# Paged key caches laid out with keys transposed, gathered page by page into the operand of the score matmuls

## The chip, the cores and the metric

The kernel runs on one core of a Trainium2 chip. The metric is the device time of one execution in microseconds (us). Several executions are timed, and their median is given; one more execution is recorded by the hardware profiler, and the rows below come from it. TensorE is called PE (its weight loads PEld), VectorE DVE, ScalarE ACT, GpSimd POOL, and SyncE SP; SP and POOL issue the DMAs.

## The reference, cut to what matters

One layer of a decoder handles a prompt of 512 tokens and 8 sample sequences of 4 new tokens, which share all weights. Two mixers run from one input projection: a gated short convolution, and sparse attention with three branches. What the change touches is the attention of the sample tokens over the paged past, and the state of the convolution:

```
rows   = cache_sel[page_table]            # 8 sequences x 8 pages x 128 tokens, keys and values, 4 heads of 64
s_s    = q . k_sel - slope * distance     # scores of the selected branch; one block of 64 tokens is masked out
o_s    = softmax(s_s) . v_sel
s_w    = q . k_win - slope * distance     # scores of the window branch over cache_win, 512 tokens
o_w    = softmax(s_w) . v_win
o      = gate0 * o_c + gate1 * o_s + gate2 * o_w
v      = bias + sum_k w[k] * up[t + k]    # up = state_conv (2 rows of 1024 channels) followed by cg * xin
```

All data are float32; `cache_sel` is (80 pages, 128 tokens, 2 x 4 x 64), `cache_win` (8, 512 tokens, 2 x 4 x 64), `state_conv` (8, 2, 1024).

## The kernel before, in words

The whole program is traced in order by `build`, and a scheduler orders each engine's queue; each engine then runs its queue in that order. Matmuls of the large projections take float32 operands that are split in a high and a low part (`split`: ACT makes `wh`, DVE makes `wl`), three matmuls for each block of 128 input channels (lines 181 to 183). The weights come through three buffers `raw` by DMAs on SP, and two buffers each of `wh` and `wl`.

After the projections of the queries (tiles `qh` and `ql`, stored to DRAM by SP), the stage of the sample attention begins. Its constants `tb` and the convolution state `st` are loaded by SP. Eight small PE transposes turn `st` into `stT`, channels on partitions (lines 727 to 733). Then two streams of work are woven together:

- the filler, `fill_gen`: for each of 8 channel blocks the three projections `cg`, `xin` and `bg` of the convolution (`conv_gen`), then three gate projections. It yields after every twelve matmuls (a step), four steps to a projection, 108 steps in all. Four of them run ahead of the sample attention.
- `sample_gen(bp)`, for each of 4 pairs of sequences. What it yields is the number of filler steps that are put in at that point.

For one pair, `sample_gen` first gathers the selected rows: one indirect DMA on POOL for each sequence (`gather`, line 789) fills a tile `sraw` of 128 partitions x 8 rows x 512, each partition with eight consecutive tokens (16 KB). There are two such buffers, and the window rows `wraw` use one of them later. The compressed scores (`sx`) give the importance `imp`, from which `mk` and the bias table `bs` follow; `bs` is made on POOL.

`branch` then does one branch of attention. `key_T` transposes the keys on PE (`kt`, line 850), 128 x 128 at a time with four transposes to a PSUM tile, and ACT or DVE copies the tile to SBUF. Four matmuls with the block diagonal queries `qbd` give the scores `ss`; `softmax_part` adds the table and takes the minimum; ACT does the exponential; DVE scales `S`; PE transposes the probabilities (`pt`), and matmuls with the value half of `sraw` or `wraw` add to `sacc`. The selected branch goes first, the window branch second; `wraw` is loaded between the two, by two DMAs on POOL. The yields of a pair add up to 27 steps.

PSUM tiles for projections and transposes share five buffers of tag `g`; scores have two buffers, the accumulator one. Small copies of the convolution (`up`, `ncv`) run on POOL.

Of the kernel before, what the change touches and what calls it, by code (L numbers as in the profile page):

```python
# [9 lines left out]
F32 = mybir.dt.float32  # L10
# [8 lines left out]
D = 1024  # L19
KC = 8  # L20
# [25 lines left out]
def _tables():  # L46
# [12 lines left out]
    offs = (p % 16)[:, None]  # L59
# [13 lines left out]
    pos = 8 * (n % 128) + n // 128  # L73
    tsel = -sl * (PAST + tt - pos)
    n = np.arange(512)
    pos = 512 + 4 * (n % 128) + n // 128
    wd = PAST + tt - pos
# [22 lines left out]
def build(tc, a, o):  # L100
# [52 lines left out]
    ixs = cst.tile([128, 8], I32, name="ixs")  # L153
# [203 lines left out]
    fidx = mp.tile([128, 12], F32, name="fidx")  # L357
# [15 lines left out]
    mk8 = tsm[:, 19:27].rearrange("p (x m) -> p x m", x=1).broadcast_to([128, 8, 8])  # L373
    dve.tensor_mul(pm_.rearrange("p (b x) -> p b x", b=8), ptf.rearrange("p (b x) -> p b x", b=8), mk8)
    dve.tensor_reduce(fidx[:, 4:12], pm_.rearrange("p (b x) -> p b x", b=8), axis=AX.X, op=ALU.add)
    dve.tensor_scalar(ixs, fidx[:, 4:12], 16.0, tsm[:, 2:3], ALU.mult, ALU.add)
# [399 lines left out]
    csv = a["cache_sel"].rearrange("n t w -> (n t w)").rearrange("(x y) -> x y", y=8 * 512)  # L776

# [7 lines left out]
    def gather(bp):  # L785
        res = []
        for b2 in range(2):
            t = srp.tile([128, 8, 512], F32, tag="sraw", bufs=2, name=nm("sraw"))
            pool.indirect_dma_start(out=t.rearrange("p j w -> p (j w)"), out_offset=None, in_=csv, in_offset=bass.IndirectOffsetOnAxis(ap=ixs[:, 2 * bp + b2:2 * bp + b2 + 1], axis=0))
            res.append(t)  # L790
        return res

    def sample_gen(bp):

        b0 = 2 * bp
        sraw = gather(bp)
# [23 lines left out]
        yield 3  # L820
# [17 lines left out]
        for jh in range(2):  # L838
            pool.tensor_tensor(bs[:, jh * 512:(jh + 1) * 512].rearrange("p (j s k) -> p j s k", j=4, s=16),
                               t_sel[:, jh * 512:(jh + 1) * 512].rearrange("p (j s k) -> p j s k", j=4, s=16),  # L840
                               mk.rearrange("p (x s y) -> p x s y", x=1, y=1).broadcast_to([128, 4, 16, 8]), op=ALU.add)
        dve.tensor_scalar_mul(px[:, 0:63], px[:, 0:63], G[:, 0:1])

        def key_T(raw, j0, which):

            res = []
            for b2, gp, rows in quads[2 * which:2 * which + 2]:
                tp = tp_ps(nm("kt"))
                for j in range(4):
                    pe.transpose(tp[:, j * 128:(j + 1) * 128], raw[b2][:, j0 + j, gp * 128:(gp + 1) * 128], ident)  # L850
                kt = smp.tile([128, 512], F32, tag="kt", bufs=4, name=nm("kt"))
                evac(kt, tp)
                res.append(kt)
            return res
# [3 lines left out]
        def branch(raw, nj, tables, xo, br, first):  # L858
# [3 lines left out]
            kts = key_T(raw, 0, 0)  # L862
            yield 1
            kts += key_T(raw, 0, 1)
            yield 1
            for q4 in range(k):
                p = s_ps(nm("ss"))
                for (b2, gp, rows), kt in zip(quads, kts):
                    pe.matmul(p[rows, :], lhsT=qbd[:, b0 + b2, gp, :], rhs=kt, start=True, stop=True)
                softmax_part(S[:, q4 * 512:(q4 + 1) * 512], p, tables[q4], nx[:, q4:q4 + 1])  # L870
                if q4 + 1 < k:
                    kts = key_T(raw, 4 * (q4 + 1), 0)
                    yield 1
                    kts += key_T(raw, 4 * (q4 + 1), 1)
                    yield 1
# [12 lines left out]
            yield 4  # L888
# [8 lines left out]
            yield 1  # L897
            for j in range(nj):
                for b2, gp, rows in quads:
                    pe.matmul(acc[rows, 0:128], lhsT=pts_[j // 4][:, (j % 4) * 128 + rows.start:(j % 4) * 128 + rows.stop],  # L900
                              rhs=raw[b2][:, j, 256 + gp * 128:256 + gp * 128 + 128], start=(first and j == 0), stop=False)
# [13 lines left out]
        yield 1  # L915
# [4 lines left out]
        yield 1  # L920
# [508 lines left out]
def _arrays(inputs):  # L1429
    arrs = {k: np.ascontiguousarray(np.asarray(inputs[k])).reshape(s) for k, s in _SHAPES.items()}  # L1430
    arrs["tab_s"], arrs["tab_a"], arrs["tab_b"] = _tables()
    return arrs
# [14 lines left out]
```

## Time and profile before

| | us |
|---|---|
| median of 3 runs | 1344.76 |
| lowest and highest of the runs | 1344.42, 1345.23 |
| profiled execution, its own time | 1343.75 |
| its span in the trace | 1342.0 |
| PE busy | 1310.5 |
| DVE, ACT, POOL busy | 654.3, 537.5, 70.3 |

The time of an execution holds a little more than the span of the trace: 1.75 us here. All points of time in the rows count from the start of the span. "Idle before" in a row is the time in which the engine did nothing ahead of the instruction, with what ended it.

### The profile page before, as it was taken

Reading aid. Unit: us, or ns where it says so; the run is one execution under the profiler, and the core shown is the slowest. Engines: PE = TensorE matmul, PEld = TensorE weight load, DVE = VectorE, ACT = ScalarE, POOL = GpSimd, SP = SyncE. Lnnn points to the kernel's source line nnn. Section 1 sums busy time; section 2 is a strip of 40 time slices with the busy share of each in tenths; the row PEclk is TensorE's granted clock in tenths of the full one; section 3 lists DMA queues with packets and bytes.
Section 4 is the critical chain, followed back from the end, with each engine's and each line's share of the span. In section 5 each row is a group of like instructions: output and inputs, shape, how many; then the busy total and the mean of one; then the engine's idle time right before and its main releaser. Section 6 shows DMA issues by size and latency. Waiting matters only on the chain.

```text
span 1342.0 us, 25662 instructions
## 1 busy us (share of the span) xinstructions
PE 1310.5 (98%) x10840; PEld 1210.6 (90%) x10840; DVE 654.3 (49%) x1570; ACT 537.5 (40%) x1065; POOL 70.3 (5%) x123
## 2 busy tenths in 40 slices
PE   7999999997999999999999999999999999999997
PEld 6788899996999999899777777999999999999996
DVE  5559332343454454426687676667433333333335
ACT  6335233432332334324776776435323223222223
POOL 2101030001011110001000000000000000000000
PEclk8999999998999999999999999999999999999999
DMA  9996036872535562754457336532223223133221
GB/s 330 313 331 231 33 112 188 275 218 83 215 130 196 185 213 95 195 132 131 124 152 199 101 110 176 155 126 64 64 64 95 95 65 124 56 87 87 87 64 67
DMA packets 138025, 193.56 MB, mean 144 GB/s; under 512 B 4818, under 2 KB 124762, under 8 KB 132919
## 3 DMA queue, kind: packets, MB, share of 16 engines
q1 hardware_dynamic: 133302, 149.98, 36.5%
q0 software_dynamic: 4608, 41.95, 8.3%
q8 instruction: 85, 1.39, 0.5%
q14 instruction: 30, 0.24, 0.1%
HBM read 174.47 MB, written 25.76 MB: 149 GB/s over the span
## 4 chain that ended last, share of the span: by engine, by line
PE 95%; DMA 2%; DVE 1%; ACT 1%; issue 0%; SPq 0%; ACTq 0%; DVEq 0%
PE lin L181 19%; PE lin L182 19%; PE lin L183 19%; PE dn L181 3%; PE dn L182 3%; PE dn L183 3%; PE acc L1133 3%; PE ptp L1139 3%; PE phi L462 2%; PE phi L460 2%; PE phi L461 2%; PE xt L446 2%; PE modp L229 2%; PE kt L850 2%; PE sp L1108 1%; PE sp L1109 1%
## 5 line engine op out<-in xcount | busy, mean ns | idle before, releaser
L181 PE MATMUL lin<-h_hi,wh 128*128 128x288 f32 (+1 forms) x1648 | 479.4, 291 | 0.0
L182 PE MATMUL lin<-h_lo,wh 128*128 128x288 f32 (+1 forms) x1648 | 475.2, 289 | 0.0
L183 PE MATMUL lin<-h_hi,wl 128*128 128x288 f32 (+1 forms) x1648 | 473.8, 288 | 0.0
L181 PEld LDWEIGHTS lin<-h_hi,wh 128*128 128x128 f32 x1648 | 311.1, 189 | 9.4 <-issue 8.1
L182 PEld LDWEIGHTS lin<-h_lo,wh 128*128 128x128 f32 x1648 | 310.7, 189 | 0.5
L183 PEld LDWEIGHTS lin<-h_hi,wl 128*128 128x128 f32 x1648 | 310.1, 188 | 0.3
L177 DVE TENSOR_TENSOR wl<-raw,wh 128x1024 fp32r<-128x1024 f32 x132 | 159.9, 1212 | 244.5 <-ACT wh L176 244.2
L176 ACT ACTIVATE wh<-raw 128x1024 fp32r<-128x1024 f32 x132 | 137.9, 1045 | 300.0 <-PE lin L182 211.4
L181 PE MATMUL dn<-f_hi,wh 128*128 128x256 f32 (+1 forms) x352 | 101.9, 290 | 0.0
L182 PE MATMUL dn<-f_lo,wh 128*128 128x256 f32 (+1 forms) x352 | 101.3, 288 | 0.0
L183 PE MATMUL dn<-f_hi,wl 128*128 128x256 f32 (+1 forms) x352 | 101.0, 287 | 0.0
L1115 ACT ACTIVATE P<-P,nms 128x512 f32<-128x512 f32 (+3 forms) x128 | 70.6, 555 | 18.8 <-DVE nms L1114 17.9
L1114 DVE CUSTOM_DVE_ANT_0 P<-sp,ta 128x512 f32<-128x512 f32 (+3 forms) x128 | 57.5, 482 | 31.0 <-PE sp L1102 23.5
L183 PEld LDWEIGHTS dn<-f_hi,wl 128*128 128x128 f32 x352 | 66.3, 188 | 0.0
L181 PEld LDWEIGHTS dn<-f_hi,wh 128*128 128x128 f32 x352 | 66.2, 188 | 0.0
L182 PEld LDWEIGHTS dn<-f_lo,wh 128*128 128x128 f32 x352 | 66.2, 188 | 0.0
L460 PE MATMUL phi<-xh,wph 128*128 128x512 f32 x128 | 54.0, 422 | 0.0
L461 PE MATMUL phi<-xh,wpl 128*128 128x512 f32 x128 | 52.1, 407 | 0.0
L462 PE MATMUL phi<-xl,wph 128*128 128x512 f32 x128 | 52.0, 408 | 0.0
L448 ACT ACTIVATE xh<-xt 128x512 fp32r<-128x512 f32 x64 | 34.8, 597 | 32.3 <-PE xt L446 31.4
L449 DVE TENSOR_TENSOR xl<-xt,xh 128x512 fp32r<-128x512 f32 x64 | 41.0, 684 | 13.1 <-ACT xh L448 13.1
L1139 PEld LDWEIGHTS ptp<-ident,P 128*128 128x128 f32 x320 | 35.7, 141 | 10.9 <-issue 8.9
(370 smaller groups left out, 2110.2 us busy)
## 6 DMA issues: line engine op xcount, KB each, us to landing
raw<-in_w_in SPq DMA_DIRECT2D x26, 1024.0 KB, 6.6
raw<-in_w_ada SPq DMA_DIRECT2D x24, 1024.0 KB, 9.3
raw<-in_w_gate SPq DMA_DIRECT2D x11, 1024.0 KB, 5.4
raw<-in_w_up SPq DMA_DIRECT2D x11, 1024.0 KB, 5.4
wraw<-in_cache_win POOLq DMA_DIRECT2D x8, 1024.0 KB, 7.0
raw<-in_w_down SPq DMA_DIRECT2D x8, 1024.0 KB, 5.7
out_new_win_sample<-in_cache_win SPq DMA_DIRECT2D x8, 1016.0 KB, 10.5
rq<-in_w_in SPq DMA_DIRECT2D x8, 512.0 KB, 12.0
```

What stands on the lines that cost most here:

```text
L176: act.activation(oh, view, AF.Copy)
L177: dve.tensor_sub(ol, view, oh.bitcast(F32))
L181: pe.matmul(p, lhsT=wh[:, k, :], rhs=xh, start=start, stop=False)
L182: pe.matmul(p, lhsT=wh[:, k, :], rhs=xl, start=False, stop=False)
L183: pe.matmul(p, lhsT=wl[:, k, :], rhs=xh, start=False, stop=stop)
L449: dve.tensor_sub(xlb[v][:, lp * 512:lp * 512 + 512], p, xo.bitcast(F32))
L460: pe.matmul(po, lhsT=w_h, rhs=mh, start=first, stop=False)
L461: pe.matmul(po, lhsT=w_l, rhs=mh, start=False, stop=False)
L462: pe.matmul(po, lhsT=w_h, rhs=ml, start=False, stop=last)
L1114: dve.tensor_tensor_reduce(out=t[:, 0:n], in0=sps[br], in1=t_dist[:, 512 - n:512], scale=-hs, scalar=3e38, op0=ALU.add, op1=ALU.min, accum ...
L1115: act.activation(t[:, 0:n], t[:, 0:n], AF.Exp, scale=-1.0, bias=nms[:, c:c + 1], accum_out=sums[:, c:c + 1])
L1139: pe.transpose(tp[:, r * 128:(r + 1) * 128], P[br, r][:, 128 * j:128 * j + 128], ident)
```

## The change

The host lays three inputs out in another way before the launch. In `cache_sel` a page keeps its 128 rows of 512 numbers, but row p of a page now holds, for two pairs of heads, component p of the keys of all 128 tokens (2 x 128 numbers), and then the 256 value numbers of token p. A new input `cache_winT` has the same for the window: 1024 key numbers by component, 1024 value numbers by token. `cache_win` stays for the copy to the output. `state_conv` comes as 128 x 128, channels on partitions.

In the kernel the state is loaded straight into `stT`, and the tile `st`, the eight transposes and the copy go. `gather` issues one indirect DMA for each page, eight for a sequence, 128 rows of 2 KB each. `key_T`, its transposes and the copies to `kt` go; the score matmuls read slices of `sraw` (four pages, 128 numbers each, 2 KB apart) and of the window tile as their moving operand. The position tables follow the new order of tokens. There are three buffers of tag `sraw` instead of two: the gather of a pair is issued in the middle of the pair before, after its selected branch, and that of the first pair ahead of the filler; the window tile of a pair is loaded by one DMA at the pair's start. The yields of a pair are set anew and add up to 24 steps.

```diff
-    ixs = cst.tile([128, 8], I32, name="ixs")
+    ixs = cst.tile([128, 64], I32, name="ixs")
...
-    mk8 = tsm[:, 19:27].rearrange("p (x m) -> p x m", x=1).broadcast_to([128, 8, 8])
-    dve.tensor_mul(pm_.rearrange("p (b x) -> p b x", b=8), ptf.rearrange("p (b x) -> p b x", b=8), mk8)
-    dve.tensor_reduce(fidx[:, 4:12], pm_.rearrange("p (b x) -> p b x", b=8), axis=AX.X, op=ALU.add)
-    dve.tensor_scalar(ixs, fidx[:, 4:12], 16.0, tsm[:, 2:3], ALU.mult, ALU.add)
+    dve.tensor_scalar(ixs, ptf, 128.0, tsm[:, 2:3], ALU.mult, ALU.add)
...
-    st = cv.tile([16, D], F32, name="st")
-    sync.dma_start(st, a["state_conv"])
     stT = cv.tile([128, 8, 16], F32, name="stT")
-    p = tp_ps("stp")
-    for k in range(KC):
-        pe.transpose(p[:, k * 16:(k + 1) * 16], st[:, k * 128:(k + 1) * 128], ident[0:16, 0:16])
-    dve.tensor_copy(stT, p[:, 0:128].rearrange("p (k n) -> p k n", k=8))
+    sync.dma_start(stT.rearrange("p k n -> p (k n)"), a["state_conv"])
...
     def gather(bp):
         res = []
         for b2 in range(2):
-            t = srp.tile([128, 8, 512], F32, tag="sraw", bufs=2, name=nm("sraw"))
-            pool.indirect_dma_start(out=t.rearrange("p j w -> p (j w)"), out_offset=None, in_=csv, in_offset=bass.IndirectOffsetOnAxis(ap=ixs[:, 2 * bp + b2:2 * bp + b2 + 1], axis=0))
+            t = srp.tile([128, 8, 512], F32, tag="sraw", bufs=3, name=nm("sraw"))
+            for pg in range(8):
+                col = (2 * bp + b2) * 8 + pg
+                pool.indirect_dma_start(out=t[:, pg, :], out_offset=None, in_=a["cache_sel"], in_offset=bass.IndirectOffsetOnAxis(ap=ixs[:, col:col + 1], axis=0))
             res.append(t)
         return res
+    rows_of = {0: gather(0)}
...
-        sraw = gather(bp)
+        sraw = rows_of.pop(bp)
+        wt = srp.tile([128, 2, 2048], F32, tag="sraw", bufs=3, name=nm("wraw"))
+        pool.dma_start(wt, a["cache_winT"][b0:b0 + 2].rearrange("b p w -> p b w"))
...
-        yield 3
+        yield 4
...
-        def key_T(raw, j0, which):
-            res = []
-            for b2, gp, rows in quads[2 * which:2 * which + 2]:
-                tp = tp_ps(nm("kt"))
-                for j in range(4):
-                    pe.transpose(tp[:, j * 128:(j + 1) * 128], raw[b2][:, j0 + j, gp * 128:(gp + 1) * 128], ident)
-                kt = smp.tile([128, 512], F32, tag="kt", bufs=4, name=nm("kt"))
-                evac(kt, tp)
-                res.append(kt)
-            return res
...
-        def branch(raw, nj, tables, xo, br, first):
+        def branch(keys, vals, nj, tables, xo, br, first, wait):
...
-            kts = key_T(raw, 0, 0)
-            yield 1
-            kts += key_T(raw, 0, 1)
-            yield 1
             for q4 in range(k):
                 p = s_ps(nm("ss"))
-                for (b2, gp, rows), kt in zip(quads, kts):
-                    pe.matmul(p[rows, :], lhsT=qbd[:, b0 + b2, gp, :], rhs=kt, start=True, stop=True)
+                for b2, gp, rows in quads:
+                    pe.matmul(p[rows, :], lhsT=qbd[:, b0 + b2, gp, :], rhs=keys(b2, gp, q4), start=True, stop=True)
                 softmax_part(S[:, q4 * 512:(q4 + 1) * 512], p, tables[q4], nx[:, q4:q4 + 1])
-                if q4 + 1 < k:
-                    kts = key_T(raw, 4 * (q4 + 1), 0)
-                    yield 1
-                    kts += key_T(raw, 4 * (q4 + 1), 1)
-                    yield 1
...
-            yield 4
+            yield wait
...
-            yield 1
+            yield 2
...
-        yield from branch(sraw, 8, [bs[:, 0:512], bs[:, 512:1024]], 64, 1, True)
-        wt = srp.tile([128, 2, 4, 512], F32, tag="sraw", bufs=2, name=nm("wraw"))
-        wr = []
-        for b2 in range(2):
-            pool.dma_start(wt[:, b2], a["cache_win"][b0 + b2].rearrange("(p j) w -> p j w", j=4))
-            wr.append(wt[:, b2])
-        yield 6
-        yield from branch(wr, 4, [t_win], 96, 2, False)
+        yield from branch(lambda b2, gp, q4: sraw[b2][:, 4 * q4:4 * q4 + 4, gp * 128:(gp + 1) * 128],
+                          lambda b2, gp, j: sraw[b2][:, j, 256 + gp * 128:384 + gp * 128],
+                          8, [bs[:, 0:512], bs[:, 512:1024]], 64, 1, True, 6)
+        if bp < 3:
+            rows_of[bp + 1] = gather(bp + 1)
+        yield from branch(lambda b2, gp, q4: wt[:, b2, gp * 512:(gp + 1) * 512],
+                          lambda b2, gp, j: wt[:, b2, 1024 + j * 256 + gp * 128:1152 + j * 256 + gp * 128],
+                          4, [t_win], 96, 2, False, 6)
...
-        yield 1
+        yield 2
...
-        yield 1
+        yield 2
```

## Rows read from the trace of the kernel before

**Rows 1.** The page: busy time and share of PE; chain that ended last, by engine.
```profile
PE 1310.5 (98%) x10840; PEld 1210.6 (90%) x10840; DVE 654.3 (49%) x1570; ACT 537.5 (40%) x1065; POOL 70.3 (5%) x123
...
PE 95%; DMA 2%; DVE 1%; ACT 1%; issue 0%; SPq 0%; ACTq 0%; DVEq 0%
```

**Rows 2.** Windows: length, busy us by engine (instructions), clock, DMA share, GB/s.
```profile
305.00:316.00 11.00, 2.30 (x25) 2.13 (x14) 3.05 (x13) 2.84 (x5) 0.20 (x1) 0.64 0.45 153
...
440.00:497.00 57.00, 56.54 (x542) 51.96 (x541) 27.99 (x74) 18.70 (x34) 6.62 (x15) 1.00 0.53 186
497.00:545.00 48.00, 45.70 (x439) 40.91 (x438) 24.23 (x55) 23.18 (x38) 3.63 (x6) 1.00 0.32 112
```

**Rows 3.** Timeline of PE at the stage's start: start, duration, instruction, idle before.
```profile
304.84 0.29 PE L807 MATMUL sx<-kn,qbd 128*32 128x64 f32 x8
313.83 1.03 PE L732 MATMUL stp<-ident,st 16*128 16x16 f32 x8 [8.70 <-DMA st<-in_state_conv]
314.80 0.61 PE L181 MATMUL lin<-h_hi,wh 128*128 128x288 f32 x1
...
318.30 0.29 PE L183 MATMUL lin<-h_hi,wl 128*128 128x288 f32 x1
318.43 0.29 PE L181 MATMUL lin<-h_hi,wh 128*128 128x288 f32 x1
```

**Rows 4.** Timelines of ACT, DVE and SP's queue over the same stretch.
```profile
298.72 1.06 ACT L176 ACTIVATE wh<-raw 128x1024 fp32r<-128x1024 f32 x1 [2.21 <-PE lin L182]
304.70 1.06 ACT L176 ACTIVATE wh<-raw 128x1024 fp32r<-128x1024 f32 x1 [2.21 <-PE lin L182]
...
313.90 0.35 ACT L816 ACTIVATE px<-sxs,n 128x63 f32<-128x63 f32 x1 [6.48 <-DVE n L779]
...
313.44 0.28 DVE L801 TENSOR_TENSOR gm<-tb,gT 48x128 f32<-48x128 f32 x1 [5.91 <-DMA tb<-in_tab_b]
...
308.44 0.39 SPq L728 DMA_DIRECT2D st<-in_state_conv  x1
```

**Rows 5.** Chain of 316 to 545 us: shares by line, and one link.
```profile
by line: PE lin L181 23.8%; PE lin L182 22.7%; PE lin L183 22.3%; PE kt L850 9.3%; PE ss L869 5.4%; DMA sraw<-in_cache_sel,ixs 5.3%; PE sacc L900 4.6%; PE pt L893 2.3%; ACT L991 0.6%; PE imp L823 0.4%; issue 0.4%; PE ptx L912 0.4%; PE sacc 
...
327.67 1.03 PE kt L850 x8
```

**Rows 6.** PE's groups of line 850, 316 to 545 us: count, busy us, mean ns, idle.
```profile
L850 PE MATMUL kt<-ident,sraw 128*128 128x128 f32 x128 | 17.1, 276 | 0.5 <-DMA sraw<-in_cache_sel,ixs 0.5
...
L850 PE MATMUL kt<-ident,wraw 128*128 128x128 f32 x64 | 8.3, 272 | 0.0
```

**Rows 7.** POOL's groups by line over the whole span, same columns.
```profile
L428 POOL DMA_INDIRECT gt<-in_cache_cmp,ixc x16 | 16.0, 1002 | 113.4 <-DVE gt L438 111.2 <-DVE ixc L372 1.8 <-issue 0.3
...
L789 POOL DMA_INDIRECT sraw<-in_cache_sel,ixs x8 | 9.7, 1213 | 19.3 <-PE ptx L912 16.8 <-issue 1.4 <-DMA k_dr1l<-kl 0.6
L839 POOL TENSOR_TENSOR bs<-tb,mk 128x512 f32<-128x512 f32 x8 | 8.5, 1075 | 25.4 <-DVE mk L836 21.5 <-PE lin L182 3.8
```

**Rows 8.** Timelines of POOL and of DVE around two indirect DMAs.
```profile
6.93 0.96 POOL L428 DMA_INDIRECT gt<-in_cache_cmp,ixc  x1 [0.30 <-issue]
...
408.57 1.87 POOL L789 DMA_INDIRECT sraw<-in_cache_sel,ixs  x1 [0.54 <-issue]
...
408.32 1.23 DVE L177 TENSOR_TENSOR wl<-raw,wh 128x1024 fp32r<-128x1024 f32 x1 [0.53 <-ACT wh L176]
```

**Rows 9.** DMA issues: count, KB each, median us from issue to landing.
```profile
k_dr1h<-kh SPq DMA_DIRECT2D x2, 256.0 KB, 2.0
...
sraw<-in_cache_sel,ixs POOLq DMA_INDIRECT x8, 11.0
```

**Rows 10.** Timelines of DVE and PE from the mask to the scaled probabilities, pair 0.
```profile
329.63 0.24 DVE L836 TENSOR_SCALAR mk<-tb,mn 128x16 f32<-128x16 f32 x1
...
338.40 1.06 PE L869 MATMUL ss<-kt,qbd 128*32 128x512 f32 x8
...
342.79 0.75 DVE L886 TENSOR_SCALAR S<-S,f 128x1024 f32<-128x1024 f32 x1
```

More of the change, by code (lines that the diff above doesn't have):

```diff
@@ L58, in _tables @@
     offc = ((p % 8) * 4)[:, None]
-    offs = (p % 16)[:, None]
+    offs = p[:, None]
     m16 = np.arange(16)[None, :] == p[:, None] // 8
@@ L72, in _tables @@
     n = np.arange(1024)
-    pos = 8 * (n % 128) + n // 128
-    tsel = -sl * (PAST + tt - pos)
+    tsel = -sl * (PAST + tt - n)
     n = np.arange(512)
-    pos = 512 + 4 * (n % 128) + n // 128
-    wd = PAST + tt - pos
+    wd = PAST + tt - (512 + n)
     twin = np.where(wd < 512, -sl * wd, NEG)
@@ L356, in build @@
     pm_ = mp.tile([128, 64], F32, name="pm_")
-    fidx = mp.tile([128, 12], F32, name="fidx")
+    fidx = mp.tile([128, 4], F32, name="fidx")
     vrow = mp.tile([104, 128], F32, name="vrow")
@@ L774, in slab_for @@
         return conv_w[nme]
-    csv = a["cache_sel"].rearrange("n t w -> (n t w)").rearrange("(x y) -> x y", y=8 * 512)
     def softmax_part(out, pin, table, nmx):
@@ L838, in sample_gen @@
         for jh in range(2):
[L839 to L841 removed]
+            pool.tensor_tensor(bs[:, jh * 512:(jh + 1) * 512].rearrange("p (s k) -> p s k", s=8),
+                               t_sel[:, jh * 512:(jh + 1) * 512].rearrange("p (s k) -> p s k", s=8),
+                               mk[:, jh * 8:jh * 8 + 8].rearrange("p (s y) -> p s y", y=1).broadcast_to([128, 8, 64]), op=ALU.add)
         dve.tensor_scalar_mul(px[:, 0:63], px[:, 0:63], G[:, 0:1])
[L844 to L854 removed]
         acc = acc_ps(nm("sacc"))
[L858 removed]
+        def branch(keys, vals, nj, tables, xo, br, first, wait):
             S = smp.tile([128, 1024], F32, tag="S", bufs=1, name=nm("S"))
@@ L900, in branch @@
                     pe.matmul(acc[rows, 0:128], lhsT=pts_[j // 4][:, (j % 4) * 128 + rows.start:(j % 4) * 128 + rows.stop],
-                              rhs=raw[b2][:, j, 256 + gp * 128:256 + gp * 128 + 128], start=(first and j == 0), stop=False)
-        yield from branch(sraw, 8, [bs[:, 0:512], bs[:, 512:1024]], 64, 1, True)
-        wt = srp.tile([128, 2, 4, 512], F32, tag="sraw", bufs=2, name=nm("wraw"))
-        wr = []
-        for b2 in range(2):
-            pool.dma_start(wt[:, b2], a["cache_win"][b0 + b2].rearrange("(p j) w -> p j w", j=4))
-            wr.append(wt[:, b2])
-        yield 6
-        yield from branch(wr, 4, [t_win], 96, 2, False)
+                              rhs=vals(b2, gp, j), start=(first and j == 0), stop=False)
+        yield from branch(lambda b2, gp, q4: sraw[b2][:, 4 * q4:4 * q4 + 4, gp * 128:(gp + 1) * 128],
[6 more added lines that the diff above has]
+                          4, [t_win], 96, 2, False, 6)
         tp = tp_ps(nm("ptx"))
@@ L1431, in _arrays @@
     arrs["tab_s"], arrs["tab_a"], arrs["tab_b"] = _tables()
+    cs = arrs["cache_sel"].reshape(80, 128, 2, 2, 128)
+    arrs["cache_sel"] = np.concatenate([cs[:, :, 0].transpose(0, 3, 2, 1).reshape(80, 128, 256), cs[:, :, 1].reshape(80, 128, 256)], axis=2).reshape(80 * 128, 512)
+    cw = arrs["cache_win"].reshape(8, 512, 2, 2, 128)
+    cv = cw[:, :, 1].reshape(8, 4, 128, 256).transpose(0, 2, 1, 3).reshape(8, 128, 1024)
+    arrs["cache_winT"] = np.concatenate([cw[:, :, 0].transpose(0, 3, 2, 1).reshape(8, 128, 1024), cv], axis=2)
+    arrs["state_conv"] = np.ascontiguousarray(arrs["state_conv"].reshape(16, 8, 128).transpose(2, 1, 0)).reshape(128, 128)
     return arrs
```

## The prediction

> **What bounds the kernel now.** I read the page's busy shares and its chain first [rows 1]. The reader is to see one engine: TensorE (PE) is busy for 1310.5 of 1342.0 us and carries 95% of the chain that ended last. So an edit pays what it takes off PE, plus the PE idle time that it closes; work taken from VectorE, ScalarE or POOL pays only through these two. Then the windows over the stage that the diff touches, the sample attention with the convolution's matmuls as filler, 305 to 545 us [rows 2]: between 305 and 316 us PE works 2.3 of 11 us, from 440 to 497 all but 0.46 us, from 497 to 545 all but 2.3 us. Third, the timelines of that hole [rows 3, 4] and the stage's chain [rows 5]. Last, the rows of what the diff multiplies, POOL's DMAs [rows 7 to 9].
>
> The hole is a DMA's. PE finishes L807 at 305.1 us, then stands 8.7 us until state_conv has landed, because the eight transposes of `st` are next in its queue; the first projection matmul follows at 314.80 us [rows 3]. That DMA was issued at 308.44 us, behind the last q stores on SP [rows 4].
>
> **The change, part by part.**
>
> *State transposes go.* The first matmul of conv 0 can follow L807: its `wh` split had run at 298.72 us [rows 4]. That is 314.80 - 305.13 = 9.7 us. The hole also left PE at its lower level: the granted clock of 305 to 316 is 0.64 [rows 2], and the fourteen matmul intervals from 314.80 to 318.30 took 3.5 us where the pace afterwards is 0.13 us each, 1.8 us [rows 3]. Without the idle time that 1.7 us goes too: 11.4 us together. What is late next? The table `tb` lands at 313.4 us as before, and `px` on ScalarE waits for it until 313.90 [rows 4]. Behind `px` in ScalarE's queue stand the copy of `cg` and the split of the `bg` weights. PE meanwhile has `cg` and `xin` (8 steps of twelve matmuls, 1.5 us each at the 0.12 to 0.13 us pace, 12 us), whose weights were split before 306 us, so it is fed until about 317; the five PSUM tiles of tag g hold the four halves of these two. `stT` now comes by the one SP DMA and is first read for `v` of conv 0, after `xin`. Bounds of this term: 11.4 us if nothing new blocks, about 0 if `cg` is blocked just as long. I take 11.4, since the releases wanted before 317 us come at 313.4 to 313.9.
>
> *Key transposes go.* 192 transposes and 48 evacuations. In the chain of 316 to 545 us they are 9.3% of 229 us, 21.3 us, in groups of eight such as the 1.03 us at 327.67 [rows 5]; one group of about 0.9 us is hidden there behind the gather's link. PE's own busy time for them is 17.1 + 8.3 = 25.4 us [rows 6]. So between 22.2 and 25.4; I take 23. All of it counts, because the filler around them is PE work as well. The evacuations cost PE nothing before (other filler ran) and return nothing.
>
> *The score matmuls stay*: the same number, at 5.4% of 229 us [rows 5], 12 groups of 1.03 us. Their moving operand is now 128-element runs 2 KB apart instead of one run. No row shows that form; lower bound 0, upper bound a doubling, 12 us. I take 0: the value matmuls already read such slices of the same tiles, and fetch no more per column.
>
> *Steps between waits.* Per pair the generator yields 24 steps instead of 27. Of 108 filler steps 104 were left, fewer than 4 x 27, so the last pair ran out of filler; 4 x 24 = 96 leaves 8. The 2.3 us of idle time in 497 to 545 us, mostly waits for `pts` and `ob` with no filler left, and the 0.46 us before [rows 2] should close but for a few tenths: 2.3 us taken together.
>
> *The gather* is where the change can lose. One indirect DMA for each sequence becomes eight, so 16 for a pair. It is issued when the previous pair's value matmuls free the tiles, and it is needed at the next pair's first score matmul. Between lie 16 steps (24 us) and about 3.4 us of the window branch and small matmuls: 27.4 us. An indirect DMA of 128 rows holds POOL 1.00 us at 8 KB a row and 1.21 us at 16 KB [rows 7], so I bound one of 2 KB a row by 0.96 and 1.87 us, the shortest and the longest that stand in [rows 8], and add 0.30 us between two in a row [rows 8]. It is nearest to the 8 KB row, 1.0 us. Then 16 x 1.3 = 21 us, and three or so stretched by 0.86 us (below), 2.6 us. The last then lands about 2 us later, as stores of the same 256 KB do, and not after the 11 us of a 2 MB one [rows 9]: some 26 us. That fits, with 1.5 us to spare. At the upper bound, 16 x 2.17 + 2 = 37 us, each of three pairs waits 9 us. I put 0.7 us for each, 2 us. Pair 0 is fetched long before. Queued behind the 16 on POOL are the small copies of `up` and `ncv`, wanted one conv (18 us) later, then the load of `wt` and `bs`, wanted later than the gather itself; those have room if it has.
>
> Why some are stretched: the 1.87 us one at 408.57 began while VectorE's L177, started at 408.32, was running [rows 8]. [...]
>
> *Shorter room for the softmax.* Without transposes the scores follow `imp` at once, and `bs` (two POOL instructions of 1.08 us [rows 7]) comes after `mk`, which ended at 329.87, 2.2 us after `imp` gave way to the first transposes at 327.67 [rows 5, 10]. From there to the scaled `S` it is what followed the scores before, 338.40 + 1.06 to 343.54 = 4.1 us [rows 10]: 2.2 + 2.2 + 4.1 = 8.5 us against 2 + 6 x 1.5 = 11 us of cover. Two foreign instructions of 1.2 us on VectorE or ScalarE use that up; from 0 to 3 us for each of four pairs, I take 0.5: 2 us. [...] Index arithmetic at the start: three small VectorE instructions become one, under the first loads: 0.
>
> **Sum.** 11.4 + 23 + 2.3 = 36.7 us off, 2 + 2 + 1 = 5 us on: 31.7 us. The profiled execution's span of 1342.0 becomes 1310.3, its time of 1343.75 (1.75 us beside the span) becomes 1312.1. It lay 1.0 us under the median of the three runs, 1344.76; so about 1313 us.
>
> **Rivals.**
> 1. *The first hole moves instead of closing.* `cg` or the split of `bg` blocks PE for as long. For it: ScalarE stood idle 6.48 us and VectorE 5.91 us for the same `tb` [rows 4]. Against: PE has 12 us of ready matmuls. Price 9 to 11 us: 1323. Chance 0.10.
> 2. *Gather or softmax a little late*, 4 to 5 us for each pair: indirect DMAs of 1.5 to 1.9 us. For it: the stretched row. Against: 1.0 us is the common one. Price 15 us: 1328. Chance 0.13.
> 3. *Slower than before: the gather is serial.* If each DMA's landing holds up the next, one costs 1.0 us of issue and 2.0 us of landing [rows 7, 9]: 48 us, 21 us late; PE waits in order, three times, 62 us in all: 1375. It decides from the point where the waits eat 31.7 us, a gather of 38 us, 2.4 us for one DMA. Against it: two gathers stood 0.30 us apart, the first long from landed [rows 8]. Chance 0.06.
> [...]
> 4. *Strided reads cost.* The doubling above: 1325. Chance 0.02. *Nothing moves*, gains and waits cancelling: 0.03.
>
> **Chances and range.** Forecast 0.66, around 1306 to 1320: all gains with no loss give 1306, and 25.4 instead of 23 another 2 less. A measurement of this kernel can tell about 0.2%, 2.7 us. Faster than that: 0.66 + 0.10 + 0.13 + 0.02 = 0.91; same 0.03; slower 0.06. The range takes in rivals 1, 2 and 4: 1303 to 1329.
>
> **What would show it.** The projection matmuls start near 305 us with no wait for state_conv, and the clock near 1.0 from there. No `kt` rows; PE busy some 25 us less. Sixteen indirect DMAs of about 1.0 us in a row on POOL, the last landing before the next `ss`; if PE waits for `sraw`, rival 2 or 3. `ss` still 1.0 us for eight. The prediction is wrong if a gather takes over 30 us, or if PE stops behind `cg`.

## The result: slower in the first comparison, near the forecast on three chips later

The comparison that answers the prediction gave 1364.35 us (1363.85 to 1364.62) for the changed kernel against 1344.86 us for the one before: a ratio of 1.0145, with a 95% interval of 1.0127 to 1.0162. The forecast was 1313 us. So both its direction and its range were missed.

The same program, without a letter changed, was run three more times beside the kernel before, on three chips: 1316.52, 1316.95 and 1316.62 us, with ratios of 0.9797 [0.9780, 0.9813], 0.9799 [0.9783, 0.9816] and 0.9795 [0.9776, 0.9815]. The kernel before took 1344.1 to 1344.9 us everywhere. It isn't known whether the chip of the first comparison is one of them. So there are two profiles of one program to read, and the question became what lies between them: 1362.5 us of span in the first, 1315.0 us in the second.

The page of the changed kernel in the first comparison: busy time and share of PE, VectorE, ScalarE and POOL, and the chain that ended last by engine.

```profile
PE 1301.3 (96%) x10640; PEld 1200.7 (88%) x10640; DVE 636.3 (47%) x1543; ACT 521.2 (38%) x1039; POOL 121.7 (9%) x175
...
PE 94%; issue 2%; DMA 1%; DVE 1%; ACT 0%; SPq 0%; DVEq 0%; ACTq 0%
```

The same two lines where it took 1316.5 us.

```profile
PE 1285.9 (98%) x10640; PEld 1190.7 (91%) x10640; DVE 636.0 (48%) x1543; ACT 521.0 (40%) x1039; POOL 122.1 (9%) x175
...
PE 96%; DMA 1%; DVE 1%; ACT 0%; issue 0%; SPq 0%; DVEq 0%; ACTq 0%
```

Beside [rows 1] the second page is the one that was forecast: 200 matmuls fewer, PE's busy time 1310.5 - 1285.9 = 24.6 us lower. (PE's eight state transposes are among the 200.) In the first, "issue" has 2% of the chain. That word means that PE waited for nothing that the profile shows. The waits of PE say how much of it there is (line, what it waited for, us in all, times, longest).

```profile
PE lin L179 <- issue: 11.9, 13, 1.6
PE lin L180 <- issue: 10.7, 13, 1.8
PE lin L181 <- issue: 6.8, 8, 1.7
PE lin L180 <- DVE yin_lo L210: 6.1, 1, 6.1
...
PE lin L179 <- ACT yin_hi L209: 1.7, 1, 1.7
...
PE pt L867 <- issue: 1.1, 2, 0.9
```

No wait names `sraw`: the gathers were not late. 11.9 + 10.7 + 6.8 + 1.1 = 30.5 us of idle time have no cause that the profile shows. The windows say where it lies (length, PE busy, and, third from the end, the granted clock). First the run of 1364 us.

```profile
229.00:252.00 23.00, 18.02 (x131) 16.75 (x128) 4.25 (x6) 5.43 (x8) 17.28 (x17) 0.93 0.82 266
252.00:280.00 28.00, 26.98 (x193) 26.18 (x193) 8.48 (x14) 11.94 (x17) 0.10 (x1) 0.88 0.83 250
330.00:385.00 55.00, 47.34 (x433) 43.68 (x430) 21.68 (x65) 11.29 (x22) 19.98 (x27) 0.91 0.53 173
385.00:440.00 55.00, 45.81 (x426) 41.17 (x425) 21.41 (x61) 13.66 (x25) 19.44 (x27) 0.91 0.53 173
440.00:497.00 57.00, 48.97 (x447) 44.36 (x446) 22.13 (x67) 13.10 (x24) 20.02 (x28) 0.91 0.51 167
```

And the run of 1316.5 us, where all five stretches are full, at full clock; three of them:

```profile
229.00:252.00 23.00, 23.00 (x199) 22.87 (x194) 7.40 (x10) 10.62 (x16) 17.31 (x18) 1.00 0.93 294
...
330.00:385.00 55.00, 55.00 (x578) 50.60 (x577) 27.36 (x78) 16.26 (x32) 22.86 (x32) 1.00 0.65 208
...
440.00:497.00 57.00, 57.00 (x563) 53.01 (x555) 26.45 (x74) 17.66 (x31) 9.51 (x20) 1.00 0.56 177
```

The four gathers lie in just these stretches (POOL's first indirect DMAs start at 230.06, 345.99, 403.44 and 461.71 us). The span differs by 1362.5 - 1315.0 = 47.5 us. Of these 30.5 us are issue idle time, and 1301.3 - 1285.9 = 15.4 us are PE busy for longer with the same 10640 matmuls: the clock reads 0.88 to 0.93 over these stretches. In short windows around the second stall it is 1.00 up to 361 us, 0.50 from 363 to 371 us and 1.00 again from 372 us; PE's first stop of over 1 us there is that before 358.08 us. The other 1.6 us are idle time elsewhere.

One stall from close by, timelines of the run of 1364 us: POOL's row of indirect DMAs, then PE.

```profile
345.99 1.05 POOL L780 DMA_INDIRECT sraw<-in_cache_sel,ixs  x1 [10.32 <-PE sacc L874]
...
357.38 0.95 POOL L780 DMA_INDIRECT sraw<-in_cache_sel,ixs  x1 [0.30 <-issue]
...
365.66 0.95 POOL L780 DMA_INDIRECT sraw<-in_cache_sel,ixs  x1 [0.30 <-issue]
```

```profile
358.08 0.28 PE L179 MATMUL lin<-h_hi,wh 128*128 128x256 f32 x1 [1.14 <-issue]
...
360.20 0.28 PE L179 MATMUL lin<-h_hi,wh 128*128 128x256 f32 x1 [1.60 <-issue]
360.92 0.28 PE L180 MATMUL lin<-h_lo,wh 128*128 128x256 f32 x1 [0.44 <-issue]
362.32 0.37 PE L181 MATMUL lin<-h_hi,wl 128*128 128x256 f32 x1 [1.12 <-issue]
363.72 0.37 PE L179 MATMUL lin<-h_hi,wh 128*128 128x256 f32 x1 [1.03 <-issue]
...
368.65 0.37 PE L180 MATMUL lin<-h_lo,wh 128*128 128x256 f32 x1 [0.33 <-issue]
```

These are plain filler matmuls; the profile shows nothing that they wait for, and at full clock they follow each other every 0.12 us. From about the ninth DMA of the row until three us after the last has begun, PE lets through one matmul, or two or three, and mostly goes on only 0.7 us or a multiple of it later (360.20, 360.92, 362.32, 363.72). The first eight disturb nothing: PE is busy for all of 345 to 355 us.

PE isn't the only engine that is late. The copy of the tile `pt` on VectorE starts at 368.84 us, 11.9 us after the last matmul that fills it; in the run of 1316.5 us it starts 0.1 us after. PE and VectorE, the run of 1364 us, then the other:

```profile
356.66 0.27 PE L867 MATMUL pt<-ident,S 128*128 128x128 f32 x1 [0.24 <-issue]
368.84 0.69 DVE L140 COPY pts<-pt 128x512 f32<-128x512 f32 x1 [6.81 <-remote]
```

```profile
345.43 0.60 PE L867 MATMUL pt<-ident,S 128*128 128x128 f32 x4
346.14 0.68 DVE L140 COPY pts<-pt 128x512 f32<-128x512 f32 x1
```

"Remote" stands where the view can name no instruction as the releaser. In the run of 1364 us VectorE and ScalarE have nine waits of this kind, 77.8 us in all; the trace of the kernel before has none.

### The profile page after: what moved, and what is told of

The parts are those of the page before. It is cut to its first block, busy times and chain, and to the rows that moved or that the text cites. A ratio compares the mean times of both kernels' runs of the same rounds, so it can differ in the third digit from the quotient of the medians.

```text
span 1362.5 us, 25289 instructions
## 1 busy us (share of the span) xinstructions
PE 1301.3 (96%) x10640; PEld 1200.7 (88%) x10640; DVE 636.3 (47%) x1543; ACT 521.2 (38%) x1039; POOL 121.7 (9%) x175
## 3 DMA queue, kind: packets, MB, share of 16 engines
q0 software_dynamic: 8512, 41.95, 9.0%
## 4 chain that ended last, share of the span: by engine, by line
PE 94%; issue 2%; DMA 1%; DVE 1%; ACT 0%; SPq 0%; DVEq 0%; ACTq 0%
PE lin L179 19%; PE lin L181 19%; PE lin L180 19%; PE dn L180 3%; PE dn L179 3%; PE dn L181 3%; PE acc L1107 3%; PE ptp L1113 3%; PE phi L457 2%; PE phi L456 2%; PE phi L455 2%; PE xt L441 2%; PE modp L227 2%; PE sp L1082 1%; PE sp L1083 1%
## 5 line engine op out<-in xcount | busy, mean ns | idle before, releaser
L179 PE MATMUL lin<-h_hi,wh 128*128 128x288 f32 (+1 forms) x1648 | 481.1, 292 | 12.0 <-issue 11.9
L180 PE MATMUL lin<-h_lo,wh 128*128 128x288 f32 (+1 forms) x1648 | 478.8, 291 | 10.7 <-issue 10.7
L181 PE MATMUL lin<-h_hi,wl 128*128 128x288 f32 (+1 forms) x1648 | 479.6, 291 | 7.0 <-issue 6.8
L179 PEld LDWEIGHTS lin<-h_hi,wh 128*128 128x128 f32 x1648 | 314.5, 191 | 19.2 <-issue 15.4
L181 PEld LDWEIGHTS lin<-h_hi,wl 128*128 128x128 f32 x1648 | 313.6, 190 | 10.4 <-issue 10.1
L175 DVE TENSOR_TENSOR wl<-raw,wh 128x1024 fp32r<-128x1024 f32 x132 | 159.1, 1206 | 251.4 <-ACT wh L174 247.5
L780 POOL DMA_INDIRECT sraw<-in_cache_sel,ixs x64 | 64.0, 999 | 51.9 <-PE sacc L874 32.5
```

Of the source, the lines that this page charges most:

```text
L175: dve.tensor_sub(ol, view, oh.bitcast(F32))
L179: pe.matmul(p, lhsT=wh[:, k, :], rhs=xh, start=start, stop=False)
L180: pe.matmul(p, lhsT=wh[:, k, :], rhs=xl, start=False, stop=False)
L181: pe.matmul(p, lhsT=wl[:, k, :], rhs=xh, start=False, stop=stop)
L780: pool.indirect_dma_start(out=t[:, pg, :], out_offset=None, in_=a["cache_sel"], in_offset=bass.IndirectOffsetOnAxis(ap=ixs[:, col:col + 1] ...
```

## The experiments

The theories. **S**: rows of indirect DMAs hold PE's issue up, by themselves. **D**: late data or bytes do it. **C**: the chip decides whether it happens at all. **L**: a second loss, in the layout, takes 7.8 us everywhere. Kernels of one line of the table ran on that chip side by side; the first comparison's chip isn't known, and each of the five stands in one line alone.

| chip | kernels, median us |
|---|---|
| A | e1_state 1332.73, e2_once 1327.18, e3_direct 1317.36, e4_spread 1344.92 |
| B | e5_eight_wait 1316.69, e6_paced 1316.31, e7_half_row 1339.68, e8_half_rows 1316.68 |
| C | e9_after_again 1316.52, e10_eight_wait_again 1317.40, e11_paced_again 1318.12, e12_cv_moved 1327.46 |
| D | e13_after_third 1316.95, e14_eight_wait_third 1316.87, e15_pause_and_nco 1308.20 |
| E | e16_after_fourth 1316.62, e17_spread_again 1317.57, e18_eight_wait_fourth 1317.22 |

**e1_state**: one part alone, on the kernel before.

```diff
-    st = cv.tile([16, D], F32, name="st")
-    sync.dma_start(st, a["state_conv"])
     stT = cv.tile([128, 8, 16], F32, name="stT")
-    p = tp_ps("stp")
-    for k in range(KC):
-        pe.transpose(p[:, k * 16:(k + 1) * 16], st[:, k * 128:(k + 1) * 128], ident[0:16, 0:16])
-    dve.tensor_copy(stT, p[:, 0:128].rearrange("p (k n) -> p k n", k=8))
+    sync.dma_start(stT.rearrange("p k n -> p (k n)"), a["state_conv"])
```

> The kernel before with one part of the change alone: conv state laid out by channel, loaded straight into stT, eight transposes and the copy gone. The prediction's first term says 11.4 us less (9.7 us of idle time and 1.7 us of slow clock), so about 1333.5 us, and no wait of PE for the state near 305 us. The rival says that the hole only moves, to the loads of tb or the first slab: between 1340 and 1345 us, with another wait of PE of several us at the same place.

Measured: 1332.73 us, ratio 0.9916 [0.9899, 0.9932], 11.6 us less than the 1344.33 us of the kernel before on this chip. The windows of this kernel show the hole of [rows 2] closed, PE busy throughout and the clock at 1.00:

```profile
305.00:316.00 11.00, 11.00 (x102) 10.77 (x101) 4.27 (x14) 3.94 (x8) 0.34 (x2) 1.00 0.46 149
```

The first term of the prediction holds to 0.2 us; the rival in which the hole moves is out. The kernel before has eight indexed DMAs (2 MB each, 13 us or more apart) and no issue wait of PE in its trace; on this chip, on which e2_once and e4_spread stalled, it took its usual 1344.33 us, and e1_state, with the same eight, took less.

**e2_once**: the gathers of pairs 1 to 3 left out. These pairs read pair 0's rows again, which stay in two tiles of their own (not in the lines below).

```diff
-        sraw = rows_of.pop(bp)
+        sraw = rows_of[0]
...
-        if bp < 3:
-            rows_of[bp + 1] = gather(bp + 1)
```

> The changed kernel, with the gather issued for pair 0 alone; pairs 1 to 3 read pair 0's rows again, so 48 of the 64 indirect DMAs are left out. If the gathers themselves hold PE up (20.7 us of idle time in the stretches 346-367, 403-424 and 461-483, and about 13 us of slow clock around them), the time falls by about 33 us to about 1331 us, and the stalls of the three later stretches are gone while that of 230-253 us stays. If the stalls come from the filler's own order or from the sample branch, they stay where they are and the time stays within 5 us of 1364 us.

Measured: 1327.18 us, ratio 0.9877 [0.9861, 0.9894]. Windows: the stall of the gather that stayed, and the place where the second was.

```profile
229.00:252.00 23.00, 19.12 (x159) 17.78 (x159) 5.26 (x9) 6.79 (x11) 16.46 (x18) 0.90 0.79 254
346.00:367.00 21.00, 21.00 (x202) 19.47 (x192) 9.09 (x21) 4.58 (x9) 1.49 (x6) 1.00 0.37 130
```

No gather, no stall; where the row of sixteen stands, PE loses 3.9 of 23 us and the clock falls to 0.90. The stalls follow the gathers and not the filler. This is read within one run; the unaltered kernel didn't run on this chip.

**e3_direct**: the same tiles, as many bytes, the same queue, without the index; the pages are read in a fixed order and not by the table.

```diff
-                pool.indirect_dma_start(out=t[:, pg, :], out_offset=None, in_=a["cache_sel"], in_offset=bass.IndirectOffsetOnAxis(ap=ixs[:, col:col + 1], axis=0))
+                pool.dma_start(t[:, pg, :], a["cache_sel"][col * 128:(col + 1) * 128])
```

> The changed kernel, with each of the 64 indirect DMAs replaced by a plain DMA of the same 128 x 2 KB on the same queue (GpSimd's) into the same place; it reads pages in fixed order, not by the page table. [...]

Measured: 1317.36 us, ratio 0.9801 [0.9785, 0.9818], on the chip on which e2_once and e4_spread stalled. POOL's group of these DMAs, the windows of the first two gathers, and the software queue:

```profile
L780 POOL DMA_DIRECT2D sraw<-in_cache_sel x64 | 34.9, 552 | 49.8 <-PE sacc L874 32.6 <-DMA sraw<-in_cache_sel 14.1 <-ACT kh L209 0.8
```

```profile
229.00:252.00 23.00, 23.00 (x186) 22.96 (x186) 7.12 (x9) 9.89 (x15) 9.36 (x17) 1.00 1.00 377
330.00:385.00 55.00, 55.00 (x578) 50.60 (x577) 26.96 (x78) 15.75 (x31) 17.62 (x37) 1.00 0.62 213
```

```profile
q0 software_dynamic: 8512, 41.95, 8.6%
```

The packets and megabytes on the queue are those of the indexed form (8512 packets, 41.95 MB there too), and moved faster (377 against 254 to 266 GB/s in 229 to 252 us). Theory D, by which the time would have stayed near 1364 us, falls: neither bytes nor packets hold PE up. What does, on this chip, has to do with the indexed form, 1.00 us of POOL for each DMA where the plain one takes 0.55 us. One rival stays: POOL stood 14.1 us in all until earlier plain DMAs had landed, where the indexed ones stand sixteen in a row, 0.30 us apart.

**e4_spread** and **e17_spread_again**: the DMAs of pairs 1 to 3 put into POOL's stream between the filler's steps.

```diff
+                def issue(t=t, pg=pg, col=col):
+                    pool.indirect_dma_start(out=t[:, pg, :], out_offset=None, in_=a["cache_sel"], in_offset=bass.IndirectOffsetOnAxis(ap=ixs[:, col:col + 1], axis=0))
+                issue() if later is None else later.append(issue)
...
                 next(fill, None)
+                if gq:
+                    gq.pop(0)()
```

> The changed kernel, with the 16 indirect DMAs of pairs 1 to 3 issued one per step of the filler instead of in a row (pair 0's stay in a row); 16 steps lie between the first and the use, so the pitch grows from 1.25 us to about 1.7 us. If a backlog of the row of 16 is what holds PE up, the three later stalls go: 20.7 us of idle time and about 13 us of slow clock less, near 1331 us. If each indirect DMA costs PE its share however it is spaced, the idle time is spread over the steps but stays, and the time stays between 1355 and 1368 us.

Measured: 1344.92 us, ratio 1.0016 [1.0000, 1.0032]. The edit didn't do what was meant: nothing makes POOL wait, so it ran ahead: in the gather of pair 2 ten DMAs in a row (but for one copy of 0.21 us), a stop of 2.46 us before its own copy of `ncv`, and six more. Windows around the ten and around the six:

```profile
396.00:412.00 16.00, 13.17 (x100) 11.57 (x93) 4.25 (x13) 2.78 (x6) 10.44 (x12) 0.91 0.71 229
412.00:424.00 12.00, 12.00 (x124) 11.02 (x123) 4.62 (x9) 2.73 (x6) 8.70 (x11) 0.83 0.57 153
```

PE stands still by the end of the ten and not in the six, with 2.83 us of idle time here, about a third of what the changed kernel lost for this gather (9.2 us in 385 to 440). The stop of POOL may itself be a child of the stall: the copy waited for VectorE's `up`, and in the stalls of the first run VectorE stood idle for 8.3 to 8.9 us ahead of that same instruction. That favours S in the form "a long row", and gave the expectation of the next runs.

> The kernel with the indirect DMAs of pairs 1 to 3 in the order of the filler's steps, which took 1345 us in the first call, with a stall in every gather. If the stall belongs to the chip or its state, this takes 1316 to 1319 us where the changed kernel takes 1316 us, with no issue idle time; if it belongs to this program, it takes 1345 us again, whatever the changed kernel does.

Measured on chip E: 1317.57 us, ratio 0.9805 [0.9789, 0.9821]; a window of it:

```profile
385.00:440.00 55.00, 55.00 (x554) 51.27 (x552) 26.99 (x74) 16.34 (x28) 27.47 (x38) 1.00 0.67 218
```

The same kernel, 27 us apart, and the difference is the stall. It belongs to the chip or to its state, and not to the program alone.

**e5_eight_wait**, **e10**, **e14**, **e18**: a copy between the two tiles of a gather.

```diff
             res.append(t)
+            if b2 == 0:
+                pool.tensor_copy(small(1, "pace"), t[:, 7, 0:1])
```

> The changed kernel, with one small GpSimd copy between the two tiles of every gather, which reads the eighth page of the first tile: the second eight indirect DMAs start when the first eight have landed (a pause of about 4 us). In the run with the DMAs issued as the queue came to them PE stood still only around the ninth and tenth of the first ten in a row, and not at all in the six behind the pause. If what counts is how many follow each other without a pause, no stall is left in any of the four stretches: about 27 us of idle time and 16 us of slow clock less, less up to 4 us for pages that now land late, so 1321 to 1327 us. If what counts is the number in the whole gather or the bytes, the stalls move behind the pause and the time stays over 1350 us.

> The kernel that waits between the first eight and the second eight indirect DMAs, once more, beside the changed kernel. If the pause removes the stall, it takes 1316 to 1320 us whatever the changed kernel does. If the chip decided, it stalls where the changed kernel does: then over 1340 us.

> The kernel with a pause between the first and the second eight indirect DMAs of each gather. Where the changed kernel takes 1316 us, this takes 1316 to 1318 us. Where the changed kernel takes 1364 us, two theories part: if PE stands still only behind more than eight of them in a row, this takes 1317 to 1327 us; if the chip holds PE up during any such gather, over 1345 us.

> The kernel with the pause once more: 1316 to 1318 us beside a changed kernel of 1316 us. Beside one of 1364 us: 1317 to 1327 us if the pause is what keeps PE running, over 1345 us if not.

Measured: 1316.69, 1317.40, 1316.87 and 1317.22 us (ratios 0.9801, 0.9804, 0.9792 and 0.9800), with no issue wait among PE's in e5 and e10, and a mean clock of 0.992 to 0.993 in the profiled execution of all four, where the first comparison's had 0.978. This looked like S confirmed until e9 took the same time without the copy. And the copy makes no pause here: POOL's timeline of e5 has it behind the eleventh DMA, with nothing to wait for.

```profile
347.84 0.95 POOL L780 DMA_INDIRECT sraw<-in_cache_sel,ixs  x1 [0.30 <-issue]
348.80 0.19 POOL L783 COPY pace<-sraw 128x1 f32<-128x1 f32 x1
349.14 0.97 POOL L780 DMA_INDIRECT sraw<-in_cache_sel,ixs  x1 [0.15 <-issue]
```

So these four say nothing of whether a pause helps where the stall is.

**e6_paced** and **e11_paced_again**: each DMA held for the last matmul of a filler step.

```diff
+                    with tc.issue_after(last_mm[0].ins):
+                        gq.pop(0)()
```

> The changed kernel, with each of the 16 indirect DMAs of pairs 1 to 3 held until the last matmul of its own filler step (pair 0's stay in a row), which really spaces them by about 1.7 us. If a backlog is what holds PE up, the later three stalls go: about 1331 us, with the stall of 230-253 us still there. If each indirect DMA has its price for PE however it is spaced, the idle time stays over 15 us in the three stretches and the time near 1355 us.

> The kernel that holds each indirect DMA of pairs 1 to 3 to its filler step, once more. Its GpSimd stream was in effect that of the kernel with the DMAs in the order of the queue, which took 1345 us in the first call, while this took 1316 us. If the wait on each DMA makes the difference, it is 1316 us again (or 1327 us with pair 0's stall) beside a changed kernel of 1364 us. If the chip decided, it falls with the changed kernel: near 1345 us where that takes 1364 us.

Measured: 1316.31 and 1318.12 us (ratios 0.9800 and 0.9808). The matmuls waited for were done early, the DMAs mostly stood 1.25 us apart as before (e6), and in the row of sixteen of pair 0, untouched here, PE didn't stall either (23.00 of 23 us busy at a clock of 1.00 in 229 to 252 us, in both runs). That was the first sign against "the program alone".

**e7_half_row** and **e8_half_rows**: half the bytes of each row, and half the rows, for pairs 1 to 3. Both keep pair 0's two tiles for all pairs (not in the lines below).

```diff
+                hw = 256 if bp else 512
+                pool.indirect_dma_start(out=t[:, pg, 0:hw], out_offset=None, in_=a["cache_sel"] if hw == 512 else a["cache_sel"].rearrange("n (s w) -> (n s) w", s=2), in_offset=bass.IndirectOffsetOnAxis(ap=ixs[:, col:col + 1], axis=0))
```

```diff
+                hp = 64 if bp else 128
+                pool.indirect_dma_start(out=t[0:hp, pg, :], out_offset=None, in_=a["cache_sel"], in_offset=bass.IndirectOffsetOnAxis(ap=ixs[0:hp, col:col + 1], axis=0))
```

> The changed kernel, with the indirect DMAs of pairs 1 to 3 fetching 1 KB for each partition instead of 2 KB (half of each row left out, from other places), the same 16 in a row with 128 rows each. If bytes make the stalls, they go or halve: 1331 to 1348 us. If the number of DMAs or of their descriptors makes them, they stay where they are: about 1364 us, PE idle about 20 us in the three stretches.

> The changed kernel, with the indirect DMAs of pairs 1 to 3 fetching 64 rows of 2 KB instead of 128 (the upper 64 partitions keep pair 0's rows), the same 16 in a row. If the number of descriptors that stand in the queue makes the stalls (8 times 128 are fine, more are not), 16 times 64 are fine too and the time is about 1331 us. If the number of DMAs makes them, they stay behind the eighth and the time is 1355 to 1364 us.

Measured: 1339.68 us (ratio 0.9966 [0.9955, 0.9978]) and 1316.68 us (0.9802). On a chip without the stall neither tells count from bytes. But e7 lost 23 us in another way, seen in PE's waits and POOL's timeline:

```profile
PE pt L868 <- DVE S L861: 15.6, 3, 5.3
```

```profile
328.47 0.95 POOL L781 DMA_INDIRECT sraw<-in_cache_sel,ixs  x1 [0.30 <-issue]
329.45 2.05 POOL L835 TENSOR_TENSOR bs<-tb,mk 128x512 f32<-128x512 f32 x2
331.65 0.97 POOL L781 DMA_INDIRECT sraw<-in_cache_sel,ixs  x1 [0.16 <-issue]
```

With the value half not rewritten, the key half was free as soon as the scores were done (the first DMA starts at 319.89 us, released by `ss`), so the next gather went into POOL's queue early, around and ahead of the mask addition `bs`; that ran late, and the softmax and PE with it. This is the prediction's "gather or softmax a little late", 15.6 us in three waits, on a small change of order.

**e9_after_again**, **e13_after_third**, **e16_after_fourth**: the changed kernel itself.

> The changed kernel once more, unaltered, beside the two kernels that had no stall. In the four runs of the call before, PE had no issue stall in pair 0's gather even where that gather was the unaltered row of 16, while the three runs of the first call that keep it had one of 5 to 6 us. If the stall belongs to the program, this run takes 1364 us again with about 30 us of issue idle time. If it belongs to the chip that the call runs on or to its state, this run may come out without it, near 1321 us (1364 less 27 idle and 16 of slow clock).

> The changed kernel again, as the standard of this call: 1364 us where the chip shows the issue stalls in the gathers, 1316 us where it doesn't.

> The changed kernel as the standard of this call: 1364 us where PE shows the issue stalls in the gathers, 1316 us where it doesn't.

Measured: the three results of the section on the result. In e9 none of PE's waits is an issue wait; in e13 PE is busy for all of 229 to 252 and 346 to 367 us; e16 took the same time. C holds: the chip, or its state at the time, decides whether there is a stall. Something is missing from the trace too. Rows of the DMA issues (count, and where there is one the median us from issue to landing): the first comparison's run, then e9's.

```profile
sraw<-in_cache_sel,ixs POOLq DMA_INDIRECT x64
```

```profile
sraw<-in_cache_sel,ixs POOLq DMA_INDIRECT x64, 4.8
```

In the stalled runs (the first, e2, e4) the landings of the gathers could not be put together; in e9, e13, e16 and e17, and in e3 on the chip of e2 and e4, they could. But chip A lacks landings without a stall as well: of the 65 groups of issues 33 have a landing in e9, e13, e16 and e17, 21 in e2, 3 in e3, none in the first run and e4; of the 48 that e1's list shows, 3. So the missing records mark the chip, most where it stalls, and the first comparison's run bears the same mark.

**e12_cv_moved**: theory L by turning two pools round.

```diff
-    srp = mkpool(cst2, "srp", side="right")
     cv = mkpool(cst2, "cv", side="right")
+    srp = mkpool(cst2, "srp", side="right")
```

> The changed kernel with the pools cv and srp opened in the other order, so that cv's tiles (among them nco, which the last stores of conv state read) lie outside the place of yin_lo. If that overlap is what makes PE wait for yin_lo and yin_hi (6.1 and 1.7 us), both waits shrink below 1 us each and the time is 6 to 8 us less than the changed kernel's in the same call. If yin waits for something else that ends at the same time, the difference is under 2 us.

Measured: 1327.46 us, 10.9 us more than the changed kernel on the same chip, though both waits for yin are gone. PE's waits and POOL's first gather:

```profile
PE ss L848 <- DMA sraw<-in_cache_sel,ixs: 12.8, 4, 6.5
```

```profile
312.84 0.98 POOL L780 DMA_INDIRECT sraw<-in_cache_sel,ixs  x1 [37.52 <-DMA q_dr1l<-ql]
```

In its new place `srp` can take the first rows only when the last stores of the q projections are out: pair 0's gather starts at 312.84 instead of some 80 us earlier, and now PE does wait for `sraw`. The program issues the same work; only addresses differ.

**e15_pause_and_nco**: e14's kernel, with `nco` alone moved.

```diff
-        nco = cv.tile([18, 512], F32, tag="nco", bufs=1, name=nm("nco"))
+        nco = srp.tile([128, 8, 512], F32, tag="sraw", bufs=3, name=nm("nco"))[0:18, 0, :]
```

> The kernel with the pause, and nco placed in a free slot of srp (outside the place of yin_hi and yin_lo), so that the split of yinf no longer waits for the last stores of conv state. If those stores are the 7.8 us of wait of PE behind the sample stage, this takes 6 to 8 us less than the kernel with the pause alone in the same call: 1309 to 1311 us where that takes 1317. If the split waits for something else as well, under 3 us less.

Measured: 1308.20 us, 8.7 us less than e14 on the same chip; ratio to the kernel before 0.9729 [0.9713, 0.9745], the best of all. The windows behind the sample stage, e9's first, then e15's:

```profile
497.00:545.00 48.00, 40.32 (x304) 39.69 (x303) 17.35 (x24) 13.27 (x20) 0.00 (x0) 0.89 0.55 144
```

```profile
497.00:545.00 48.00, 46.98 (x374) 46.35 (x373) 19.18 (x27) 15.46 (x23) 0.00 (x0) 1.00 0.69 173
```

L holds: of 7.7 us of idle time in this window 6.7 go, and the clock reads 1.00 instead of 0.89.

## Why the prediction was wrong

**The step that failed** is the gather's. It asked whether POOL and the landing would be in time (26 of 27.4 us), and gave PE's own matmuls, "16 steps (24 us)", the part of the cover: that they run undisturbed beside sixteen indirect DMAs was taken without a row, and what the DMAs cost PE stands in the sum at nothing. In the first comparison they didn't: PE lost 30.5 us of issue time and 15.4 us of clock in and around the four stretches where the DMAs stand in a row. Shown: the stall is there with the gathers and gone without them (e2), and gone with plain DMAs of as many bytes on the same chip (e3). Shown too: on chips B to E it isn't there, on three of them for the very same program (e9, e13, e16), on E for e4's too (e17). No rival had it. The serial gather of rival 3 came nearest in time (1375) and is wrong in mechanism: PE never waited for `sraw`.

**What stays open** is what the chip does. The trace has only PE's "issue", VectorE's late starts and the missing landings. Whether the index or the unbroken row matters isn't told apart either. No run here was made without records, so whether the recording has a part in the stall isn't known. Whether eight in a row are safe, or a true pause helps, wasn't reached: no later chip stalled.

**Steps that held**, read in runs without the stall. The state: 11.6 us measured for 11.4 (e1). The key transposes: PE's busy time 24.6 us less, for "some 25". Strided scores: `ss` takes 7.7 + 4.2 = 11.9 us in all, no more than the 12.4 us (5.4% of 229 us) of [rows 5]; groups of line 848 on PE between 305 and 545 us in e9:

```profile
L848 PE MATMUL ss<-sraw,qbd 128*32 128x512 f32 x64 | 7.7, 598 | 0.0
L848 PE MATMUL ss<-wraw,qbd 128*32 128x512 f32 x32 | 4.2, 592 | 0.0
```

The gather: the first of sixteen begins at 335.62 us, the last at 354.86, and with the median of 4.8 us from issue to landing it is there at 359.7: 24 us for the 26 foretold. The term was mis-shaped inside: the longest of that row took 1.25 us, so there was little stretching, while the landing, taken as 2 us, was 4.8 from the issue. The stretching itself is as the prediction read it: in the run of 1364 us three DMAs (230.06, 237.02 and 359.89 us) that began while VectorE's L175 still had 0.79, 0.77 and 0.59 us to run took 1.65, 1.58 and 1.42 us, where the common one took 0.95. The waits put on the other side of the sum, 2 + 2 + 1 us, didn't come: PE has no wait at all between 300 and 500 us in e9. The last of them, 1 us for the semaphores of sixteen DMAs instead of two, was the author's figure alone; no run shows it.

**The term that was missing**: as the program reads, the third `sraw` buffer pushes the pool `cv` under the place of `yin_hi` and `yin_lo`, and their split waits for the last stores of `nco`; e12 and e15 show that the wait goes when the place changes. In e9 that wait stands in the view of the tile yin_lo, and in PE's waits:

```profile
  DMA out_new_conv_sample<-nco: 4.5, 1
```

```profile
PE lin L180 <- DVE yin_lo L210: 6.0, 1, 6.0
...
PE lin L179 <- ACT yin_hi L209: 1.7, 1, 1.7
```

The sum beside the runs: 1344.11 - 1316.52 = 27.6 us were gained on chip C. With 11.6 measured for the state and 8.7 for nco (e15 against e14), 27.6 - 11.6 + 8.7 = 24.7 us are left for the keys and the stage's end, where 23 + 2.3 were foretold; no run has these two alone. The forecast of 31.7 off was right to 4 us there, but by luck in part: an omission of 8.7 and a caution of 5 stand against each other.

## What to carry to other kernels

Cutting one DMA into many indexed ones may not be paid on POOL alone: look in the trace whether the busiest engine's "issue" time grows while they run (30.5 us in the first comparison, none in e9), and where addresses are known, the plain form moved the same 41.95 MB without it (e3). When a program's time is far off with no wait that the program explains, run it again on another chip before the program is changed; two profiles of one program (spans of 1362.5 and 1315.0 us) showed in two windows what no edit had. A pool that grows moves its neighbours: look which tiles the next stage puts on the same addresses, and what their last reader is, a store above all (8.7 us here, e15).

## What the runs showed of the hardware

- Sixteen indirect DMAs of 128 x 2 KB in a row, 1.25 us apart, let PE issue only a few matmuls (one to five) at a time in the first run, mostly 0.7 us or a multiple of it apart, from about the ninth on, and VectorE started 11.9 us after PE had filled its input. Each gather cost 6 to 9 us of PE's idle time (windows of the first run: 4.98 + 1.02, 7.66, 9.19 and 8.03 us), and the clock read 0.88 to 0.93 around it. On four of the five chips of the table (1316.3 to 1318.1 us, but for e7, e12 and e15) no such stall was seen, on B in variants of the kernel alone.
- On POOL a plain DMA of 256 KB takes 0.55 us (e3) and an indexed one 1.00 us (first run, e9), with the same 8512 packets on the queue. That they differ for the other engines is what e3 points to, with the rival named there: in 229 to 252 us PE is busy for all 23.00 us in e3, and for 19.12 and 17.24 us of them in e2 and e4 on the same chip.
- An indirect DMA that began while VectorE ran a tensor_tensor took longer on POOL by a little less than what that instruction still had to run (0.79, 0.77 and 0.59 us left: 0.70, 0.63 and 0.47 us longer, first run). The 64 plain ones of e3, in a program with the same VectorE instructions, took 0.55 us on average.
